# Rebuilding a hybrid decoder layer as a pipeline over four 512-token blocks on eight Trainium2 cores

## The chip, the cores and the metric

The kernel runs on the eight NeuronCores of one Trainium2 (trn2) chip. Each core owns 2048 of the 16384 tokens and also reads the 2048 tokens before its own (the halo), so no core talks to another. The metric is the device time of one launch in microseconds (us), taken as the time of the slowest core. Cores 0 to 3 are one die, cores 4 to 7 the other.

Executions fall in two states. In most, all cores agree within about one per cent (1124.3 to 1131.0 us in the profiled run of the old kernel). In some, the cores of a die run at a lower granted TensorE clock and the time is some per cent longer (in one run of e1 cores 0 to 3 took 1353 to 1369 us at 0.78 to 0.79, cores 4 to 7 1232 to 1247 us at 0.90); such a run is called slow. The engines are named as in the profile: PE is TensorE's matmul, PEld its weight load, DVE VectorE, ACT ScalarE, POOL GpSimd, SP SyncE.

## The reference, cut to what matters

```python
D_MODEL = 1024; SEQ = 16384; HEAD_DIM = 64
ATTN_GROUPS = ((128, 1), (512, 4), (2048, 16))  # (window, dilation) per head group
HEADS_PER_GROUP = 4                             # 12 heads, q, k, v each 768 wide
POOL_WINDOWS = (2, 4, 8, 16)                    # POOL_WIDTH = 256
FFN_HIDDEN = 2816

# one layer, cut
h = rms_norm(x, g_pre_mix[l])
proj = h @ w_in[l]                 # q, k, v (768 each), u (256), gates (2 x 1024)
q = apply_rope(q); k = apply_rope(k)
# ... per group: causal band of 129 positions inside each residue stream, softmax;
#     head j of the three groups is combined, weighted by softmax denominators
o_attn = jnp.sum(wts[..., None] * jnp.stack(outs, axis=0), axis=0)      # 256 wide
y_pool = multiscale_pool(u, w_pool_mix[l], pool_scale[l])               # 256 wide
merged = gate_a * (o_attn @ w_proj_attn[l]) + gate_p * (y_pool @ w_proj_pool[l])
x = x + rms_norm(merged @ w_out[l], g_post_mix[l])
h2 = rms_norm(x, g_pre_ffn[l])
gu = h2 @ w_gate_up[l]
x = x + rms_norm((jax.nn.silu(a) * b) @ w_down[l], g_post_ffn[l])
```

The combination over groups is the same as summing, over the three groups, the unnormalised outputs and the denominators, and dividing once at the end. Both kernels do that. The matmul operands are bf16, accumulation is in f32.

## The kernel before

It works stage by stage over all 2048 tokens, with a barrier of all engines after most stages: the halo is loaded, normalised, transposed and projected while the core's own tokens are loaded; then q and k with rope; then pooling and v; then attention; then the softmax normalisation; the gated merge; the output projection; and the feed-forward network (FFN). Each operation is given its waits by hand.

The statistics of a tile are issued one or two tiles ahead (`lag`) of its scaled copy, and while own tokens are processed the reciprocal root is taken off GpSimd (`rstd_mode["act"]`):

```python
def rstd_chain(ev_ss, col):
    if rstd_mode["act"]:
        e1 = act.op(lambda e: e.activation(out=msA[:, col:col + 1], in_=ssA[:, col:col + 1], func=AF.Sqrt, scale=1.0 / D, bias=EPS), waits=[ev_ss])
        return dve.op(lambda e: e.reciprocal(out=rsA[:, col:col + 1], in_=msA[:, col:col + 1]), waits=[e1])
    e1 = pool.op(lambda e: e.tensor_scalar(out=msA[:, col:col + 1], in0=ssA[:, col:col + 1], scalar1=1.0 / D, scalar2=EPS,
                                           op0=ALU.mult, op1=ALU.add), waits=[ev_ss])
    e2 = pool.op(lambda e: e.tensor_tensor(out=rsA[:, col:col + 1], in0=msA[:, col:col + 1], in1=nhalf[:, :], op=ALU.pow), waits=[e1])
    return e2

def norm_transpose_tile(ev_ld, gvec, dst, dst_col, idx):
    xb = idx % pa_nxb[0]
    xin = xst[xb]
    col = ss_col[0] % 48
    ss_col[0] += 1
    ev_sq = sq_accum(xin[:, :], col, [ev_ld])
    ev_rs = rstd_chain(ev_sq, col)
    n = pa_state["n"]
    pa_state["n"] += 1
    pa_state["q"].append((xin, xb, col, ev_rs, gvec, dst, dst_col, n % 2, n))
    while len(pa_state["q"]) > pa_state["lag"]:
        pa_stage2(pa_state["q"].pop(0))

hTh = P.sb("hTh", [128, 8, 2048], BF16, R_Q)
phase_a(xh, HT // 128, gpre, hTh, pq_from=9, nxb=NXB_MAX, lag=2)      # NXB_MAX = 10 tiles of x
# ... (cut)
pa_state["all_act"] = True
rope_state["qb_dve"] = True
rstd_mode["act"] = True
phase_a(xo, NT, gpre, hT, between=between)
```

Rope uses a matmul with a rotation matrix, then two VectorE products and one GpSimd sum. Attention is a unit per group, stream quarter and head, two units in flight:

```python
for slot in range(4):
    # ... (cut): the score matmuls have 64 rows, 128 columns
    pe.op(lambda e, slot=slot, qs=qs, kc=kc, g=g, p0=p0, pr=pr, bC=bC: e.matmul(ps[:, bC, slot * 128:(slot + 1) * 128], lhsT=kT[g][p0:p0 + 64, pr, kc],
                                                      rhs=qT[p0:p0 + 64, 2 * g + pr, qs], start=True, stop=True), signal=False)
    # ... (cut): the same for the previous block
ev_ec = act.op(lambda e, ub=ub, bC=bC: e.activation(out=PTc[ub][:, :], in_=ps[:, bC, :], func=AF.Exp, scale=0.125),
               waits=[evs, pt_free[ub]])
# ... (cut)
ev_mc = dve.op(lambda e, ub=ub: e.tensor_tensor(out=PTc[ub][:, :], in0=PTc[ub][:, :], in1=masks[:, MC, :], op=ALU.mult), waits=[ev_ec])
# ... (cut)
att_q.append((g, s_, h, ub, ev_mc, ev_mp))
while len(att_q) > 2:
    att_finish(att_q.pop(0))
```

The reciprocal of the denominators is taken as ln and exp on one row per head, split into a high and a low bf16 part and spread over 64 partitions by matmuls with a row of ones (`norm_rows`, `norm_apply`, `norm_pack`).

The softmax here doesn't subtract the row's maximum and nothing guards it: scores larger than these inputs give would overflow.

## Time and profile before

The median is 1132.49 us (two runs, 1131.86 and 1133.12). The view of the whole span first: three rows of the table of 40 equal slices (28.3 us each). A digit is the busy share in tenths; PEclk is the granted TensorE clock in tenths of full speed; DMA is the busy share of the DMA engines.

```profile
PE   2568899999799779999999599999999999999993
PEclk9989899989655559999999789999999999999997
DMA  8996100000000123522088466666333544440231
```

TensorE is at 90% or more in most slices; the exceptions are the first five (the load), three 7s from the start of attention to the normalisation, the 5 at the end of the output projection, and the last slice. Where PEclk shows 5 TensorE is busy but at half clock. The table of stretches of the same core, cut where the lines of code change, gives the stages. The columns are: stretch, its length, then busy us (and instructions) of PE, PEld, DVE, ACT, POOL, the granted clock, the DMA share and GB/s.

```profile
0.00:125.00 125.00, 71.78 (x548) 51.22 (x548) 72.64 (x119) 65.89 (x105) 46.35 (x72) 0.94 0.80 200
125.00:222.00 97.00, 94.46 (x424) 41.81 (x425) 60.44 (x92) 27.70 (x47) 77.91 (x45) 0.97 0.07 23
222.00:290.00 68.00, 62.17 (x466) 48.66 (x464) 19.19 (x22) 26.83 (x63) 22.21 (x8) 0.95 0.00 1
290.00:390.00 100.00, 92.89 (x768) 75.79 (x768) 71.89 (x129) 63.55 (x118) 0.00 (x0) 0.51 0.00 1
390.00:423.00 33.00, 21.35 (x48) 6.86 (x48) 23.28 (x28) 14.94 (x8) 18.44 (x8) 0.50 0.28 49
423.00:566.00 143.00, 140.38 (x640) 63.08 (x640) 41.48 (x65) 39.51 (x65) 48.12 (x47) 0.98 0.26 45
566.00:651.00 85.00, 68.43 (x384) 33.07 (x384) 39.16 (x32) 51.69 (x80) 62.18 (x83) 0.89 0.71 217
651.00:1131.00 480.00, 459.04 (x2112) 207.02 (x2112) 81.30 (x104) 71.65 (x121) 83.24 (x112) 0.98 0.45 94
```

The reader should see where there is something to gain. Attention (290 to 390) keeps TensorE busy but at clock 0.51; the normalisation (390 to 423) likewise, with 21 us of work in 33; the load (0 to 125) has 72 us of matmul in 125. Rope, merge and FFN are already dense at nearly full clock (0.97 to 0.98). The half clock is visible in single instructions. Two lines of the timeline (start us, duration us, engine, line, operation, tiles, sizes) from the attention stage show score matmuls of 128 columns that start 0.10 to 0.11 us apart:

```profile
300.01 0.31 PE L808 MATMUL ps<-qT_62,kT_17_59 64*128 64x128 bf16 x1
300.11 0.31 PE L810 MATMUL ps<-qT_62,kT_17_59 64*128 64x128 bf16 x1
```

### The profile page before, as it was taken

Reading aid. Unit: us, or ns where it says so; the run is one execution under the profiler, and the core shown is the slowest. Engines: PE = TensorE matmul, PEld = TensorE weight load, DVE = VectorE, ACT = ScalarE, POOL = GpSimd, SP = SyncE. Lnnn points to the kernel's source line nnn. Section 1 sums busy time; section 2 is a strip of 40 time slices with the busy share of each in tenths; the row PEclk is TensorE's granted clock in tenths of the full one; section 3 lists DMA queues with packets and bytes.
Section 4 is the critical chain, followed back from the end, with each engine's and each line's share of the span. In section 5 each row is a group of like instructions: output and inputs, shape, how many; then the busy total and the mean of one; then the engine's idle time right before and its main releaser. Section 6 shows DMA issues by size and latency. Waiting matters only on the chain.

```text
span 1131.0 us, 15270 instructions; the slowest of 8 cores (1124.3 to 1131.0 us)
## 1 busy us (share of the span) xinstructions
PE 1010.5 (89%) x5388; PEld 527.5 (47%) x5388; DVE 409.4 (36%) x589; ACT 361.8 (32%) x604; POOL 358.4 (32%) x373
## 2 busy tenths in 40 slices
PE   2568899999799779999999599999999999999993
PEld 1336544359688524444444244444444444444441
DVE  3557566632269772232336412111111121111110
ACT  6535333234775532222247611111111111111110
POOL 3344288805000154323268611111133200000332
PEclk9989899989655559999999789999999999999997
DMA  8996100000000123522088466666333544440231
GB/s 274 219 221 154 55 20 19 1 1 1 2 1 2 19 40 60 89 38 38 1 251 244 157 114 117 115 117 114 57 112 112 130 75 75 77 77 14 95 114 71
DMA packets 32874, 98.79 MB, mean 87 GB/s; under 512 B 4832, under 2 KB 5152, under 8 KB 32800
## 3 DMA queue, kind: packets, MB, share of 16 engines
q0 software_dynamic: 15376, 42.08, 22.3%
q1 hardware_dynamic: 16704, 55.71, 15.3%
q8 instruction: 44, 0.72, 0.3%
q14 instruction: 30, 0.25, 0.1%
q10 hardware_dynamic: 720, 0.03, 0.0%
HBM read 123.10 MB, written 16.78 MB: 124 GB/s over the span
## 4 chain that ended last, share of the span: by engine, by line
PE 79%; DMA 5%; issue 4%; DVE 4%; ACT 4%; POOL 3%; ACTq 0%; SPq 0%; DVEq 0%; POOLq 0%
PE ps L1165 13%; PE ps L1141 13%; PE ps L1144 13%; PE ps L463 9%; PE ps L564 5%; PE ps L949 5%; PE ps L952 5%; DMA sin_43_85<-sint 2%; PE ps L775 2%; PE ps L808 2%; PE ps L810 2%; PE ps L777 2%; PE ps L1009 1%; DVE hTh_92 L411 1%; PE ps L958 1%
## 5 line engine op out<-in xcount | busy, mean ns | idle before, releaser
L1165 PE MATMUL ps<-wdn_133,ffT_151 128*128 128x512 bf16 x704 | 152.3, 379 | 1.9 <-DVE ffT_151 L1149 1.9
L1165 PEld LDWEIGHTS ps<-wdn_133,ffT_151 128*128 128x128 bf16 x704 | 68.8, 98 | 85.4 <-issue 2.8
L463 PE MATMUL ps<-hT_58,wqk_64 128*128 128x512 bf16 x384 | 92.7, 387 | 1.7 <-DVE hT_58 L411 1.7
L1149 DVE TENSOR_TENSOR ffT_151<-ps,sa_113_155 128x512 bf16<-128x512 f32 x44 | 30.4, 691 | 123.0 <-PE ps L1144 123.0
L1149 DVE TENSOR_TENSOR ffT_151<-ps,sa_114_156 128x512 bf16<-128x512 f32 x44 | 30.4, 692 | 121.8 <-PE ps L1144 121.8
L1148 ACT ACTIVATE sa_114_156<-ps 128x512 f32<-128x512 f32 x44 | 26.3, 597 | 125.6 <-PE ps L1141 125.6
L1148 ACT ACTIVATE sa_113_155<-ps 128x512 f32<-128x512 f32 x44 | 26.3, 597 | 121.1 <-PE ps L1141 121.1
L1009 PE MATMUL ps<-wout_131,mT_122 128*128 128x512 bf16 x256 | 58.9, 387 | 2.7 <-POOL mT_122 L970 2.7
L463 PEld LDWEIGHTS ps<-hT_58,wqk_64 128*128 128x128 bf16 x384 | 38.0, 99 | 48.6 <-issue 5.4
L365 POOL TENSOR_SCALAR msA_53<-ssA_52 128x1 f32<-128x1 f32 x64 | 12.1, 190 | 141.6 <-ACT junk_0_105_147 L383 82.5
L1141 PE MATMUL ps<-hT_58,wgu_110_152 128*128 128x512 bf16 x224 | 52.9, 379 | 0.6 <-DMA wgu_110_152<-wgu 0.6
L1141 PE MATMUL ps<-hT_58,wgu_112_154 128*128 128x512 bf16 x224 | 52.9, 379 | 0.0
L1144 PE MATMUL ps<-hT_58,wgu_111_153 128*128 128x512 bf16 x224 | 52.9, 379 | 0.0
L1144 PE MATMUL ps<-hT_58,wgu_112_154 128*128 128x512 bf16 x224 | 52.9, 379 | 0.0
L1141 PE MATMUL ps<-hT_58,wgu_111_153 128*128 128x512 bf16 x224 | 52.9, 379 | 0.0
L1144 PE MATMUL ps<-hT_58,wgu_110_152 128*128 128x512 bf16 x224 | 52.9, 379 | 0.0
L383 ACT ACTIVATE junk_0_105_147<-ps 128x1024 bf16<-128x1024 f32 x23 | 23.3, 1012 | 85.6 <-PE ps L1165 73.8
L564 PE MATMUL ps<-wvr_65,hT_58 128*128 128x256 bf16 x384 | 42.1, 273 | 0.0
L564 PEld LDWEIGHTS ps<-wvr_65,hT_58 128*128 128x128 bf16 x384 | 40.5, 119 | 1.7
L1009 PEld LDWEIGHTS ps<-wout_131,mT_122 128*128 128x128 bf16 x256 | 24.9, 99 | 31.8 <-issue 5.4
L367 POOL TENSOR_TENSOR rsA_54<-msA_53,nhalf_55 128x1 f32<-128x1 f32 x64 | 35.5, 554 | 9.9 <-POOL msA_53 L365 0.8
L74 POOL DMA_DIRECT2D wpa_105<-wpa x1 | 0.6, 574 | 117.6 <-DVE onesb_121 L856 117.6
(272 smaller groups left out, 1895.4 us busy)
## 6 DMA issues: line engine op xcount, KB each, us to landing
wgu_112_154<-wgu POOLq DMA_DIRECT2D x14, 512.0 KB, 5.3
wgu_110_152<-wgu POOLq DMA_DIRECT2D x14, 512.0 KB, 5.3
wgu_111_153<-wgu POOLq DMA_DIRECT2D x14, 512.0 KB, 5.3
wdn_133<-wdn POOLq DMA_DIRECT2D x22, 256.0 KB, 6.1
xin_93_135<-x1s SPq DMA_DIRECT2D x8, 512.0 KB, 4.3
out<-x1b_97_139 SPq DMA_DIRECT2D x8, 512.0 KB, 2.9
xin_94_136<-x1s SPq DMA_DIRECT2D x8, 512.0 KB, 4.1
out<-x1b_98_140 SPq DMA_DIRECT2D x8, 512.0 KB, 2.9
```

The source lines that it names most:

```text
L367: e2 = pool.op(lambda e: e.tensor_tensor(out=rsA[:, col:col + 1], in0=msA[:, col:col + 1], in1=nhalf[:, :], op=ALU.pow), waits=[e1])
L383: ev = act.op(lambda e: e.activation(out=jl[k][:, :], in_=in_ap, func=AF.Square, accum_out=ssA[:, col:col + 1]), waits=list(waits) + [st[" ...
L463: ev = pe.op(lambda e, k=k: e.matmul(ps[:, bank, 0:n], lhsT=wfn(k), rhs=rhsfn(k), start=(k == 0), stop=(k == 7)), signal=(k == 7))
L564: ev = pe.op(lambda e, k=k: e.matmul(ps[:, bank, 0:256], lhsT=tok_ap_fn(k), rhs=wv_tile[:, g, k, :], start=(k == 0), stop=(k == 7)), signa ...
L949: e1 = pe.op(lambda e, k=k, wb=wb, b1=b1, tok=tok: e.matmul(ps[:, b1, :], lhsT=wgs[wb][:, 0, k, :], rhs=hT[:, k, tok], start=(k == 0), sto ...
L952: e2 = pe.op(lambda e, k=k, wb=wb, b2=b2, tok=tok: e.matmul(ps[:, b2, :], lhsT=wgs[wb][:, 1, k, :], rhs=hT[:, k, tok], start=(k == 0), sto ...
L1009: ev = pe.op(lambda e, k=k, hf=hf, pr_=pr_: e.matmul(ps[:, pr_[0] + hf, :], lhsT=mT[:, k, i * 128:(i + 1) * 128], rhs=wout[:, k, hf * 512: ...
L1141: e1 = pe.op(lambda e, k=k, wbuf=wbuf, ba=ba, tok=tok: e.matmul(ps[:, ba, :], lhsT=wbuf[:, 0, k, :], rhs=hT[:, k, tok], start=(k == 0), st ...
L1144: e2 = pe.op(lambda e, k=k, wbuf=wbuf, bb=bb, tok=tok: e.matmul(ps[:, bb, :], lhsT=wbuf[:, 1, k, :], rhs=hT[:, k, tok], start=(k == 0), st ...
L1148: es = act.op(lambda e, ub=ub, ba=ba: e.activation(out=sa[ub][:, :], in_=ps[:, ba, :], func=AF.Silu), waits=[e1, sa_free[ub]])
L1149: ef = dve.op(lambda e, ub=ub, bb=bb, j=j, b=b: e.tensor_tensor(out=ffT[:, j, b * 512:(b + 1) * 512], in0=ps[:, bb, :], in1=sa[ub][:, :], ...
L1165: ev = pe.op(lambda e, j=j, h2=h2, pr_=pr_, il=il: e.matmul(ps[:, pr_[0] + h2, :], lhsT=ffT[:, j, il * 128:(il + 1) * 128], rhs=wdn[:, j, ...
```

## The change

The intent is to mix what is starved (attention) with what is dense (projections, gates, merge), so that TensorE always has dense matmuls to run while ScalarE and VectorE work on the softmax, and to drop the barriers, the rotation matmuls and the serial normalisation. The core's own tokens come first, then the halo; the dilation-16 group, which needs all tokens, is woven with the first block's projections; then attention of block s is woven with the projections of block s+1, the pooling of block s and the merge of block s−1. Rope keeps the two halves of a head in separate tiles, so it needs four products and two sums but no matmul; a score is the sum of two matmuls over 32 rows, one per half. Waits are no longer written by hand: a helper records what each operation reads and writes and derives them.

The full diff replaces most of the file; this is its core, added lines only, with cuts marked. What is removed are the stages described above.

```diff
+def weave(main, fill):
+
+    tm = sum(c for c, _ in main) or 1e-9
+    tf = sum(c for c, _ in fill)
+    fi = 0
+    done_f = 0.0
+    done_m = 0.0
+    for c, fn in main:
+        fn()
+        done_m += c
+        while fi < len(fill) and done_f + fill[fi][0] / 2 <= tf * done_m / tm:
+            fill[fi][1]()
+            done_f += fill[fi][0]
+            fi += 1
+    while fi < len(fill):
+        fill[fi][1]()
+        fi += 1
  ... (cut)
+    def rstd(ss, rs):
+        pool.tensor_scalar(out=ss, in0=ss, scalar1=D * EPS, scalar2=None, op0=ALU.add)
+        pool.tensor_tensor(out=rs, in0=ss, in1=nhalf[:, :], op=ALU.pow)
  ... (cut)
+    def x_stat(i):
+        ss, rs = stat_slot()
+        act.activation(out=junk[:, :], in_=xst[i % 4][:, :], func=AF.Square, accum_out=ss)
+        rstd(ss, rs)
+        sq[i] = rs
+
+    def x_trans(i):
+        xb = xsb[i % 2]
+        act.activation(out=xb[:, :], in_=xst[i % 4][:, :], func=AF.Copy, scale=sq[i])
  ... (cut: the rest of x_trans: eight transposes, then one VectorE evacuation into hT or hTh)
+    def rope(banks, wa, wb, rhs, tab, dst_a, dst_b, view, n=512, t0=0):
+
+        ba, bb = banks.get(), banks.get()
+        pA, pB = ps[:, ba, 0:n], ps[:, bb, 0:n]
+        cos, sin = tab[:, 0, t0:t0 + n], tab[:, 1, t0:t0 + n]
+        ts = [rt[i][:, 0:n] for i in range(4)]
+        mm8(ba, n, wa, rhs)
+        dve.tensor_tensor(out=ts[0], in0=pA, in1=cos, op=ALU.mult)
+        dve.tensor_tensor(out=ts[1], in0=pA, in1=sin, op=ALU.mult)
+        mm8(bb, n, wb, rhs)
+        dve.tensor_tensor(out=ts[2], in0=pB, in1=sin, op=ALU.mult)
+        dve.tensor_tensor(out=ts[3], in0=pB, in1=cos, op=ALU.mult)
+        pool.tensor_tensor(out=dst_a, in0=view(ts[0]), in1=view(ts[2]), op=ALU.subtract)
+        pool.tensor_tensor(out=dst_b, in0=view(ts[1]), in1=view(ts[3]), op=ALU.add)
  ... (cut)
+    x_stat(0)
+    for i in range(2 * NT):
+        if i + 1 < 2 * NT:
+            x_stat(i + 1)
+        x_trans(i)
+        if i + 4 < 2 * NT:
+            x_load(i + 4)
  ... (cut: after each tile: up to two waiting q/k/v units are issued)
+    def att_qk(pair, items, mask):
+
+        pt = PT[pt_i[0] % 2]
+        pt_i[0] += 1
+        n_it = len(items)
+        for j, (kf, qf, c0, n) in enumerate(items):
+            for half in range(2):
+                for hh in range(2):
+                    h = 2 * pair + hh
+                    pe.matmul(ps[:, S_b + hh, c0:c0 + n], kf(half, h), qf(half, h), start=(half == 0), stop=(half == 1),
+                              signal=(j == n_it - 1 and half == 1 and hh == 1), skip_group_check=True)
+        act.activation(out=pt[:, :, :], in_=ps[:, S_b:S_b + 2, :], func=AF.Exp, scale=0.125)
+        dve.tensor_tensor(out=pt[:, :, :], in0=pt[:, :, :], in1=masks[:, mask, :].unsqueeze(1).to_broadcast([128, 2, 512]), op=ALU.mult)
+        return pt
  ... (cut)
+        def fin(pair, n, pt, pv):
+            att_pv(pair, pt, pv, n == 0)
+            if n == 3:
+                a = acc[:, s, 2 * pair:2 * pair + 2, :]
+                dve.tensor_tensor(out=a, in0=ps[:, O_b:O_b + 2, :], in1=a, op=ALU.add)
+                od = oT2[s % 2]
+                for hh in range(2):
+                    h = 2 * pair + hh
+                    vals, sums = (slice(0, 64), slice(64, 128)) if hh == 0 else (slice(64, 128), slice(0, 64))
+                    dve.reciprocal(out=rec[vals, :], in_=acc[sums, s, h, :])
+
+                    dve.scalar_tensor_tensor(out=od[vals, pair, :].rearrange("p (j rho) -> p rho j", rho=4), in0=acc[vals, s, h, :].rearrange("p (rho j) -> p rho j", rho=4),
+                                             scalar=0.5, in1=rec[vals, :].rearrange("p (rho j) -> p rho j", rho=4), op0=ALU.mult, op1=ALU.mult)
+
  ... (cut: u_units: the shifted sums of pooling, in the four blocks)
+            b = fb.get()
+            pe.matmul(ps[:, b, :], wmixb[:, c, :], zT[:, :], start=True, stop=True)
+            act.activation(out=yp[s % 2][:, c, :], in_=ps[:, b, :], func=AF.Copy, scale=pscale[:, c:c + 1])
+        return [(1.8, lambda: proj(0)), (1.8, lambda: proj(1)), (0.1, lambda: sums(0)), (0.1, lambda: sums(1))]
  ... (cut)
+    def wg_load():
+        n = wg_n[0]
+        if n < 32:
+            pool.dma(wgs[n % 2][:, :, :, :], wg_d[n % 8], d_wg[n % 2])
+            wg_n[0] += 1
  ... (cut)
+    weave(g2_main(), f1_units(0, fb))
  ... (cut)
+    for s in range(4):
+        f = []
+        if s < 3:
+            f.append(f1_units(s + 1, fb))
+        f.append(u_units(s))
+        if s > 0:
+            f.append(m_units(s - 1))
+        weave(att_main(s), mix(*f))
  ... (cut)
+    for hf in range(2):
+        pool.dma(wout[:, 4 * hf:4 * hf + 4, :], wout_d[:, 4 * hf:4 * hf + 4, :], d_wo[hf])
  ... (cut)
+    weave(m_units(3), w_units(0, 8, fb))
```

## The prediction

> **What bounds the kernel now.** The table of stretches of the slowest core splits 1131 us (stages cut where the lines change in the timeline) into: input norm, transposes and halo projections 0–125; q/k projections with rope 125–222; pooling and v 222–290; attention 290–390; softmax normalisation 390–423; gated merge 423–566; output projection 566–651; FFN 651–1131. In rope, merge and FFN TensorE is the limit: a 512-column matmul every 0.216 us at granted clock 1.0 (8 take 1.73 us in the chain). These gain nothing. The first 80 us are DMA-bound (DMA share about 1.0, 205–313 GB/s). Attention is TensorE at half clock (granted 0.50, 128-column matmuls 0.106 us apart) with VectorE nearly as full (36.9 of 40 us; 1.05 us accumulation plus 2 x 0.425 us masks a unit). Normalisation is a serial row chain (ln and exp 1.9 us each on one partition). The output projection has 55 us of matmul in 85 us.
>
> [...] the FFN's first eight matmuls take 3.57 us, later ones 1.73.
>
> **Removed:** 48 rotation matmuls in the rope stage (10 us) and their ScalarE copies; hi/lo broadcast and pack matmuls and row chain (33 us stage); all barriers; most idle TensorE around attention. **Added:** scores become two 32-row halves, 672 matmuls against 384; rope has four VectorE products (0.69 us each) instead of a copy and two; its four temporaries are single-buffered behind two 2.1 us GpSimd adds. **Moved:** own tokens first, then halo; attention woven with q/k/v, pool and merge matmuls; output projection woven with merge and FFN.
>
> **Estimate, TensorE stream at full clock from the 0.216 us matmul:**
> - Load phase: 27 MB at the 235–245 GB/s of the first 80 us is about 115 us, with only four x buffers; then about 28 us tail of halo v and last k/v. About 143 us (this includes 41 us of own q/k/v work).
> - Woven attention: 4 x 20.8 (q/k/v) + 16 (pool) + 3 x 34.5 (merge) + 48 x 1.28 (scores and values) = 264 us. Group-2 steps have little dense fill, so clock perhaps 0.75 there: 295 us.
> - Last merge plus half the output projection: 66 us, plus about 22 us of bubbles: wout's load is issued only after the last attention block; the FFN's first weights and hidden tile 7 wait for a norm chain of about 12 us.
> - FFN 456 us plus second half of the output projection 32 us, load hiccups 5, final norm and store 12.
>
> Sum 1026. Tail and bubbles may overlap more than I count, and the pairs of 32-row score matmuls on different row groups may run side by side ([...] this trace shows none), which would save up to 20 us. Central value 1005 us: gains about 70 us in attention and normalisation, 45 in load/rope/pool, 10–20 in output projection; FFN unchanged.
>
> **What would show it:** stretches: FFN half of 44 units 152 us and down 76 us as before; granted clock above 0.9 in woven blocks with merge fill, lower in the first (group 2) block; TensorE idle mostly in the first 115 us, before the output projection and before the FFN; waits there for DMA wout/wgu and for x tiles.
>
> **What would make it wrong:** half clock through group 2 and block 0 (up to +70 us); VectorE stalled in order behind GpSimd's rope adds, starving PSUM banks; on the other side, a load phase under 110 us and no bubbles (down to 950).
>
> Predicted 1005 us, 8 in 10 between 962 and 1055. Faster by over 2%: 0.95; within 2%: 0.04; slower: 0.01.

The sum stands as 1026 (its terms add to 1031, see below); the central value of 1005 takes off some 20 us, for overlap of tail and bubbles and for 32-row score matmuls that run side by side. No trace that the prediction had showed these doing so, and it does not say how their 20 us were worked out; the trace after shows 16 of them in 0.55 us. The clock of 0.75 in group 2 is an estimate of which it gives no working either; it lies between the 0.51 of attention and the 0.98 of the merge in the table above.

## More of the kernel before

The gate weights are loaded once, eight loads of 512 KB, because each is used for all four token blocks in turn; `wout` is loaded during the merge, in eight slices behind the second gate load. The pool-mix matmuls are issued behind the 48 v projections, so the VectorE and GpSimd sums that they need have that time to finish.

## The result, and the profile after

The new kernel takes 1289.06 us (median of two runs, 1285.66 and 1292.45), against 1132.49: the ratio is 1.1385, with a 95% interval from 1.1312 to 1.1458. It is slower by 14%. Here and below the ratios and intervals are worked out from the fast runs; they differ by up to 0.002 from the quotient of the medians (here 1.138). The result is correct.

The same three rows, one slice being 32.3 us here:

```profile
PE   1545566988639858776748959997999999999994
PEclk9777566778869888897977979998999999999997
DMA  8324932003012221333445754544983244442122
```

The first seven slices, where the old kernel was dense from the fourth on, are half empty, and the DMA digits drop to 3 and 2 in the second and third: the DMA engines are mostly idle there, so their rate is not the limit. (HBM reads rose from 123.10 to 150.37 MB, by the page. The 24 more gate loads of 512 KB account for 12.6 MB of that; where the rest comes from was not looked into.) The table of stretches, with the new kernel's stages: the load of own and halo tokens (two halves), group 2 and the four blocks in four pieces, the output projection, the FFN.

```profile
0.00:128.00 128.00, 55.11 (x264) 26.92 (x264) 43.02 (x52) 39.77 (x56) 52.11 (x76) 0.81 0.47 126
128.00:256.00 128.00, 88.33 (x544) 63.13 (x544) 36.73 (x48) 43.65 (x78) 35.73 (x44) 0.66 0.40 94
256.00:362.00 106.00, 83.74 (x788) 50.65 (x782) 62.76 (x63) 45.72 (x57) 34.19 (x20) 0.82 0.14 25
362.00:468.00 106.00, 72.86 (x452) 36.63 (x452) 61.35 (x68) 22.67 (x36) 34.55 (x28) 0.86 0.26 42
468.00:574.00 106.00, 77.62 (x462) 38.08 (x462) 61.00 (x62) 23.32 (x37) 32.56 (x26) 0.86 0.25 45
574.00:681.00 107.00, 64.73 (x372) 29.29 (x373) 66.47 (x60) 23.16 (x33) 20.18 (x22) 0.79 0.38 78
681.00:771.00 90.00, 70.55 (x342) 31.73 (x342) 30.38 (x31) 34.60 (x55) 46.32 (x57) 0.88 0.60 149
771.00:1290.00 519.00, 492.09 (x2304) 224.44 (x2304) 101.33 (x120) 97.29 (x161) 109.79 (x140) 0.97 0.44 99
```

No engine is full in any of the first six stretches: VectorE's largest share is 66 of 107 us, TensorE's 84 of 106. So the loss is in waits, and the view of the waits says which. For PE in the first 245 us (engine, tile awaited, line; us in total, times, longest):

```profile
PE ps L94 <- ACT xsb_30_72 L92: 70.1, 15, 8.8
PE ps L94 <- ACT xsb_29_71 L92: 31.8, 8, 15.7
```

and for PE from 256 to 672 us:

```profile
PE ps L92 <- DVE zT_112 L92: 59.2, 7, 15.5
PE ps L94 <- DVE PT_53_95 L92: 14.0, 5, 10.2
PE ps L94 <- DMA wgs_55_97<-wg: 13.4, 4, 4.7
```

**The load phase.** `xsb` is the scaled copy of an x tile, waiting to be transposed. Why does it come late? The timeline of one round:

```profile
66.69 1.90 POOL L92 TENSOR_TENSOR q_19_61<-rt_48_90,rt_50_92 128x512 bf16<-128x512 f32 x1 [9.15 <-DVE rt_50_92 L92]
68.54 1.90 POOL L92 TENSOR_TENSOR q_19_61<-rt_49_91,rt_51_93 128x512 bf16<-128x512 f32 x1
...
70.77 0.57 POOL L92 TENSOR_TENSOR rs_53<-ss_52,nhalf_51 128x1 f32<-128x1 f32 x1
...
71.44 1.15 ACT L92 ACTIVATE xsb_30_72<-xst_23_65,rs_53 128x1024 bf16<-128x1024 f32 x1 [10.45 <-POOL rs_53 L92]
72.73 0.90 PE L94 MATMUL ps<-ident_43,xsb_30_72 128*128 128x128 bf16 x7 [6.89 <-ACT xsb_30_72 L92]
```

The bracket is the idle time before the instruction and what ended it. The copy needs the reciprocal root `rs`; that is a GpSimd operation of 0.57 us which stands in GpSimd's queue behind the two rope sums, 1.90 us each; those wait for VectorE's products, which wait for matmuls, which stand in TensorE's queue behind the transposes of the tile before. The statistics run one tile ahead, the rope units come every second tile, and work runs in the order of its queue (shown for GpSimd at the end of this paragraph), so the round closes on itself. These copies (every second tile) start at 43.30, 56.72, 71.44, 84.45, 100.29 and 114.23: 14 us for two tiles of 512 KB each. The trace shows the order of GpSimd's queue: the work for `rs` runs only after both sums, from 70.40 us, although the square sum that it needs was read out on ScalarE by 58.91, before the sums began at 66.69.

Could it be the x tiles that come late? The waits of ScalarE in the first 256 us say no. It waits 95.6 us for `rs` (77.1 in the first line below, 18.5 for the other copy buffer), but for x tiles only 14.8, all of it in the first 28 us (the second line is the largest part):

```profile
ACT xsb_30_72 L92 <- POOL rs_53 L92: 77.1, 9, 11.6
ACT junk_73 L92 <- DMA xst_22_64<-xo: 7.6, 1, 7.6
```

**The woven blocks.** `zT` is the input of the pool-mix matmul. VectorE's timeline before the longest of the seven waits:

```profile
371.42 3.35 DVE L92 RECIPROCAL rec_113<-acc_56 64x512 f32<-64x512 f32 x1
374.88 1.28 DVE L92 SCALAR_TENSOR_TENSOR oT_0_62_104<-acc_56,rec_113 64x512 bf16<-64x512 f32 x1
376.19 3.35 DVE L92 RECIPROCAL rec_113<-acc_56 64x512 f32<-64x512 f32 x1
...
380.97 0.71 DVE L92 TENSOR_TENSOR uY_110<-uX_67_109 128x527 f32<-128x527 f32 x1
...
387.22 0.58 PE L92 MATMUL ps<-zT_112,wmixb_50 128*128 128x512 bf16 x1 [15.53 <-DVE zT_112 L92]
```

Two reciprocals and two products of a head pair, then the pooling sums, then the matmul: it is issued directly behind them, and everything behind it on TensorE waits too, for 15.53 us. The group of reciprocals, as the page has it (busy us, mean ns, idle before):

```profile
L92 DVE RECIPROCAL rec_113<-acc_56 64x512 f32<-64x512 f32 x16 | 53.6, 3347 | 1.1
```

54 us of VectorE that the prediction did not price at all.

**The clock.** The granted clock is 0.66 in the second stretch, and 0.69 from 350 to 400 us: it is low in the stretches where the longest waits are 8.8 to 15.7 us, and it recovers to 0.97 in the FFN. In the 2.5 us after a wait for `zT` it was 0.50 to 0.57 six times, after waits of 4.6 to 15.5 us, and 1.00 twice, after waits of 1.8 us. The length of the wait does not settle it: after six waits for the gate weights it was 0.52 to 0.64 four times (1.7, 2.6, 2.9 and 4.7 us) and 1.00 twice (2.7 and 3.4 us). Nor are waits the whole of it: in the old kernel's attention the clock was 0.50 from 300 to 340 us, where the profile has TensorE busy for all 40 us.

**What came as predicted.** The 32-row score matmuls do run side by side. Two lines of the timeline after, in a dense stretch: eight of the sixteen matmuls of one step, in two groups of four,

```profile
404.73 0.28 PE L94 MATMUL ps<-q_1_41_83,k_1_38_80 32*128 32x128 bf16 x4
404.85 0.27 PE L94 MATMUL ps<-q_1_41_83,k_2_39_81 32*128 32x128 bf16 x4
```

and the next operation's first matmul starts at 405.28: 16 matmuls in 0.55 us, 34 ns each, where 128 columns one after the other, scaled from the measured 0.216 us for 512 columns, would take about 54 ns each (my estimate from that duration). In the same trace value matmuls of 128 rows and 128 columns do start 57 ns apart (the eighth at 294.20 us, the first at 293.80, clock 1.00).

### The profile page after: what moved, and what is told of

Read it like the earlier page. It is cut to its first block, busy times and chain, and to the rows that moved or that the text cites. A ratio compares the mean times of both kernels' runs of the same rounds, so it can differ in the third digit from the quotient of the medians.

```text
span 1290.6 us, 14962 instructions; the slowest of 8 cores (1275.2 to 1290.6 us)
## 1 busy us (share of the span) xinstructions
PE 1005.0 (78%) x5520; PEld 500.9 (39%) x5520; DVE 463.0 (36%) x502; ACT 330.2 (26%) x511; POOL 365.4 (28%) x410
## 3 DMA queue, kind: packets, MB, share of 16 engines
HBM read 150.37 MB, written 16.78 MB: 130 GB/s over the span
## 4 chain that ended last, share of the span: by engine, by line
PE 63%; DVE 11%; DMA 8%; POOL 6%; issue 6%; ACT 6%; DVEq 0%; ACTq 0%; POOLq 0%; SPq 0%
PE ps L94 56%; PE ps L92 7%; DVE rec_113 L92 4%; DMA wgs_55_97<-wg 2%; DMA wgs_54_96<-wg 2%; POOL k_20_62 L92 1%; DMA wout_115<-wout 1%; DVE zT_112 L92 1%; ACT xsb_30_72 L92 1%; DVE rt_50_92 L92 1%; ACT junk_73 L92 1%; DMA xst_22_64<-xo 1%; POOL rs_53 L92 1%; DMA pscale_47<-pscale 1%; POOL q_19_61 L92 1%
## 5 line engine op out<-in xcount | busy, mean ns | idle before, releaser
L94 PE MATMUL ps<-wdna_133,ffT_132 128*128 128x512 bf16 x512 | 115.7, 379 | 0.0
L94 PE MATMUL ps<-hT_54,wgu_87_129 128*128 128x512 bf16 x420 | 102.7, 385 | 3.4 <-DMA wgu_87_129<-wgu 3.4
L94 PE MATMUL ps<-hT_54,wgu_88_130 128*128 128x512 bf16 x420 | 100.4, 379 | 0.0
L94 PE MATMUL ps<-hT_54,wgu_89_131 128*128 128x512 bf16 x392 | 94.5, 381 | 0.0
L94 PEld LDWEIGHTS ps<-wdna_133,ffT_132 128*128 128x128 bf16 x512 | 50.1, 98 | 60.4
L94 PE MATMUL ps<-hT_54,wgs_55_97 128*128 128x512 bf16 x224 | 60.7, 417 | 15.0 <-DMA wgs_55_97<-wg 14.4
L92 POOL TENSOR_SCALAR ss_52<-ss_52 128x1 f32<-128x1 f32 x80 | 17.8, 222 | 180.6 <-ACT junk_85_127 L92 118.3
L92 ACT ACTIVATE junk_85_127<-ps 128x1024 bf16<-128x1024 f32 x32 | 32.7, 1021 | 138.6 <-PE ps L92 138.6
L94 PE MATMUL ps<-ident_43,xsb_30_72 128*128 128x128 bf16 x112 | 13.3, 288 | 70.1 <-ACT xsb_30_72 L92 70.1
L94 PE MATMUL ps<-hT_54,wgs_54_96 128*128 128x512 bf16 x224 | 61.4, 419 | 6.8 <-DMA wgs_54_96<-wg 6.7
L94 PEld LDWEIGHTS ps<-hT_54,wgu_87_129 128*128 128x128 bf16 x420 | 41.5, 99 | 54.1 <-issue 6.6
L92 PE MATMUL ps<-zT_112,wmixb_50 128*128 128x512 bf16 x8 | 4.1, 506 | 73.0 <-DVE zT_112 L92 73.0
L94 PEld LDWEIGHTS ps<-hT_54,wgu_88_130 128*128 128x128 bf16 x420 | 41.0, 98 | 49.1
L94 PEld LDWEIGHTS ps<-hT_54,wgu_89_131 128*128 128x128 bf16 x392 | 38.5, 98 | 46.4 <-issue 1.1
L92 DVE RECIPROCAL rec_113<-acc_56 64x512 f32<-64x512 f32 x16 | 53.6, 3347 | 1.1
L92 DVE TENSOR_TENSOR ffT_132<-ps,sa_93_135 128x512 bf16<-128x512 f32 x30 | 20.8, 692 | 86.9 <-PE ps L92 86.9
L92 POOL TENSOR_TENSOR rs_53<-ss_52,nhalf_51 128x1 f32<-128x1 f32 x80 | 45.4, 567 | 16.3 <-DVE nhalf_51 L92 4.6
L92 DVE TENSOR_TENSOR ffT_132<-ps,sa_94_136 128x512 bf16<-128x512 f32 x29 | 20.1, 692 | 82.1 <-PE ps L92 82.1
L92 DVE TENSOR_TENSOR ffT_132<-ps,sa_95_137 128x512 bf16<-128x512 f32 x29 | 20.1, 691 | 80.7 <-PE ps L92 80.7
L92 DVE TENSOR_TENSOR PT_53_95<-PT_53_95,masks_44 128x1024 bf16<-128x1024 bf16 x24 | 34.0, 1418 | 17.6 <-ACT PT_53_95 L92 17.6
L94 PE MATMUL ps<-wdnb_134,ffT_132 128*128 128x512 bf16 x160 | 39.8, 379 | 0.0
L92 ACT ACTIVATE sa_94_136<-ps 128x512 f32<-128x512 f32 x29 | 17.3, 597 | 87.4 <-PE ps L92 87.4
```

Source lines behind the costliest of these rows:

```text
L92: self.ops.append(lambda e: getattr(e, method)(*args, **kw).then_inc(sem, 1))
L94: self.ops.append(lambda e: getattr(e, method)(*args, **kw))
```

## The experiments

All are edits of the new kernel. The first four each test one suspected cause alone; the rest build up. A gain is quoted as the difference of two ratios to the old kernel, times 1132 us, because the calls ran on different chips and each had its own runs of the old kernel (medians of the fast ones 1131.9, 1132.9, 1132.3 and 1131.7). By the intervals, a gain over the new kernel, of which there are only two runs, is sure to about 9 us, and one between two later runs to 3 or 4 us. For the stages, single profiles are compared: three edits that don't touch the load phase (e2, e3, e4) still show its end, the first exponential, at 252 to 253 us in place of 256, so differences of 4 us there mean nothing.

The two theories: **(T)** the loss is in-order waiting that the new order of issue created, in places that can be named (the x-tile round, the pool-mix matmul, the reciprocals, the weight loads), and the woven plan is sound; **(R)** the plan itself is at fault: the load phase is DMA-bound or limited by its four x buffers, and the woven blocks are limited by the total work of VectorE or by the half clock, so mending single waits brings little.

### e1_stat: statistics two tiles ahead

```diff
+    x_stat(1)
-        if i + 1 < 2 * NT:
-            x_stat(i + 1)
+        if i + 2 < 2 * NT:
+            x_stat(i + 2)
```

> The square sum and rstd of an x tile are issued two tiles ahead instead of one. Theory A (the load phase of about 250 us is a loop through the in-order queues: transposes wait for ScalarE, which waits for the GpSimd rstd that stands behind the rope adds of the previous projection, which stand behind the projection's matmuls, 14 us for two tiles): the loop is broken, two tiles take about 8 us, the load phase falls to about 170 us and the total by 60 to 90 us. Rival B (the load phase is limited by DMA or by having only four x buffers): no more than 15 us change.

Measured: ratio 1.106 (1.1038 to 1.1082), 37 us less than the new kernel; the first exponential starts at 218 us in place of 256. The direction is right, the size is a miss. The page shows a second round that the first had hidden. ScalarE in the halo half of this run:

```profile
111.94 0.38 ACT L92 ACTIVATE v<-ps 128x256 bf16<-128x256 f32 x1 [1.32 <-PE ps L92]
112.22 1.05 ACT L92 ACTIVATE junk<-xst 128x1024 bf16<-128x1024 f32 x1
...
113.25 1.14 ACT L92 ACTIVATE xsb<-xst,rs 128x1024 bf16<-128x1024 f32 x1
```

The next tile's square (`junk`) and this tile's copy (`xsb`) stand behind the evacuation of a v projection, which waits for TensorE, which has that projection behind the transposes of the tile before. So the copy too has to be issued ahead of the units (e5). In this run ScalarE also waits 36 us for x tiles after the first have landed, so rival R has some part in what is left.

### e2_late: the pool-mix matmul issued later

```diff
+    zT1 = P.sb("zT1", [128, 512], BF16, take(KB))
+    zTs = [zT, zT1]
...
+        def mixmm(c):
             b = fb.get()
-            pe.matmul(ps[:, b, :], wmixb[:, c, :], zT[:, :], start=True, stop=True)
+            pe.matmul(ps[:, b, :], wmixb[:, c, :], zTs[c][:, :], start=True, stop=True)
...
-        return [(1.8, lambda: proj(0)), (1.8, lambda: proj(1)), (0.1, lambda: sums(0)), (0.1, lambda: sums(1))]
+        return [(1.0, lambda: proj(0)), (1.0, lambda: proj(1)), (0.1, lambda: sums(0)), (0.1, lambda: sums(1)),
+                (2.0, lambda: mixmm(0)), (0.6, lambda: mixmm(1))]
```

> The pool-mix matmul of a block is issued some 10 us of fill work after the sums that feed it, with a second zT buffer, instead of straight behind them. Theory A (TensorE stands in order at this matmul, 73 us in all in the trace of the changed kernel, most of it lost, and the clock falls to half after each): 50 to 75 us faster. Rival B (the woven blocks are bound by VectorE, busy 15 to 20 of 25 us in many stretches, so the idle time only moves): under 20 us.

Measured: 1.1066 (1.1039 to 1.1093), 36 us less. This is less than theory A's 50 to 75 us and more than the rival's 20: part of the wait was real loss, part only moved. All waits for `zT` are gone, 59 us of them in the woven blocks and 14 just after, and 36 come back as time. The rest turned into other waits: TensorE now waits 31 us for the gated products `tg` in these blocks, where it waited 11 before, and 18 us for `wout`, where it waited 4.

### e3_copy: reciprocals replaced by copies (wrong result)

```diff
-                    dve.reciprocal(out=rec[vals, :], in_=acc[sums, s, h, :])
+                    dve.tensor_copy(out=rec[vals, :], in_=acc[sums, s, h, :])
```

> Wrong result on purpose: each of the 16 reciprocals of 64x512 (3.35 us each, 53.6 us of VectorE) becomes a copy. Theory A (VectorE's long instructions hold up the bank releases and the pool sums behind them): 20 to 40 us faster, because part of the wait on zT goes with it. Rival B (VectorE is off the critical path): under 8 us.

Measured: 1.0912 (1.0894 to 1.0931), 54 us less. The sixteen copies take 0.422 us each against 3.347, an eighth, so 46.8 us of VectorE work were removed, and the time fell by about as much (54 with an uncertainty of 9): this work is on the critical path almost one to one, although VectorE is busy only about 60% of the woven stretches. The gain was more than expected, and about half of it may be the wait for `zT`, which falls from 73 to 48 us in this run.

### e4_wgs3: a third buffer for the gate weights

```diff
-    wgs = [P.sb("wgs%d" % i, [128, 2, 8, 128], BF16, R2 + i * 4 * KB) for i in range(2)]
+    wgs = [P.sb("wgs%d" % i, [128, 2, 8, 128], BF16, (R2 + i * 4 * KB) if i < 2 else R2 + 43 * KB + 256) for i in range(3)]
...
-            if j == 1 and wg_n[0] == m_n[0] + 1:
+            if j == 1 and wg_n[0] == m_n[0] + 2:
```

> A third buffer for the gate weights, loaded two units ahead. Theory A (about 20 us of TensorE waits on the gate weights' DMA, and slow clock after each, 4.4 per cent of the chain): 15 to 40 us faster. Rival B (the waits only stand in for VectorE or pool waits that follow): under 8 us.

Measured: 1.1265 (1.1177 to 1.1353), an interval that overlaps the new kernel's own (1.1312 to 1.1458); its fast runs were 1266.9 and 1283.88, the other two were slow. Inconclusive by itself: the gain lies between nothing and some 25 us. The profile of the faster run does show the wait itself gone: 21.1 us for the gate weights in the new kernel, none here.

### e5_ahead: statistics two tiles ahead, scaled copy one tile ahead

```diff
+    def x_copy(i):
+        act.activation(out=xsb[i % 2][:, :], in_=xst[i % 4][:, :], func=AF.Copy, scale=sq[i])
...
+        if i + 1 < 2 * NT:
+            x_copy(i + 1)
+            if i + 5 < 2 * NT:
+                x_load(i + 5)
         x_trans(i)
-        if i + 4 < 2 * NT:
-            x_load(i + 4)
```

(on top of e1)

> As e1_stat, and the scaled copy of an x tile is also issued one tile before its transposes. e1's trace showed a second loop in the halo half of the load phase: ScalarE's square and copy of the next tile stand behind the evacuations of the two v projections, which stand behind the transposes that need the copy, 6.9 us a tile. If the remaining loss of the load phase is this loop (theory A), the first score exponential starts at about 165 us or earlier, against 218 in e1 and 256 in the changed kernel, and the total is 40 to 60 us below e1 (about 1200). If it is DMA or the four x buffers (rival B), it starts after 205 and the total is within 15 us of e1.

Measured: 1.0809 (1.078 to 1.0838), 65 us less than the new kernel, 28 less than e1. The first exponential starts at 191.7 us. The order of issue alone, with the same four x buffers and the same bytes, shortens the load phase from 256 to 192 us; so neither the DMA rate nor the number of buffers set the 256, and rival R falls as the main cause in this phase. (A copy issued earlier also frees its x buffer earlier, so the loads start sooner; the run doesn't separate this.) It did not come down as far as expected, 165 us: TensorE still waits 53 us for `xsb`, and ScalarE 60 us for `rs`.

### e6_late: e5 and e2 together

The edit is that of e2, on top of e5.

> e5 and the late pool-mix matmul of e2. If load phase and woven blocks are separate losses, the 35 us of e2 add to e5 in full; if both only move the work to a shared limit, less than 20.

Measured: 1.0532 (1.0509 to 1.0555), 31 us less than e5. Alone (e2) the same edit gave 36: the two causes lie in different stages and add nearly in full.

### e7_rec: one reciprocal for two heads, with the right result

```diff
-                a = acc[:, s, 2 * pair:2 * pair + 2, :]
-                dve.tensor_tensor(out=a, in0=ps[:, O_b:O_b + 2, :], in1=a, op=ALU.add)
...
-                    dve.reciprocal(out=rec[vals, :], in_=acc[sums, s, h, :])
...
+                    dve.tensor_tensor(out=rec[vals, :], in0=ps[sums, O_b + hh, :], in1=acc[sums, s, h, :], op=ALU.add)
+                    dve.tensor_tensor(out=val[vals, :], in0=ps[vals, O_b + hh, :], in1=acc[vals, s, h, :], op=ALU.add)
+                dve.reciprocal(out=rec[:, :], in_=rec[:, :])
```

(then one product for both heads; on top of e6)

> e6 and one reciprocal for two heads instead of two (right result): 7.4 us of VectorE a pair instead of 10.5 by the durations of the trace, 25 us less over 8 pairs. If VectorE limits the woven blocks (e3 gave back 54 us for 54 us of reciprocals less about 6 of copies), 20 to 30 us faster than e6; if e3's gain was mostly the wait of the pool-mix matmul, which e6 has already taken away, under 10.

Measured: 1.0292 (1.0275 to 1.031), 27 us less than e6, as expected, and correct. VectorE's busy time falls by 24.6 us (460.3 to 435.7), so its work counts about one to one here too, with the wait for `zT` already gone. The group of reciprocals in this run:

```profile
L92 DVE RECIPROCAL rec<-rec 128x512 f32<-128x512 f32 x8 | 26.8, 3353 | 0.2
```

128 partitions cost what 64 did (3353 ns against 3347), so putting the denominators of two heads side by side halves the cost.

### e8_early: the output-projection and first FFN weights loaded early, in large pieces

```diff
+        if s == 3:
+            d_wo = [dsem("d_wo%d" % i) for i in range(2)]
+            for hf in range(2):
+                pool.dma(wout[:, 4 * hf:4 * hf + 4, :], wout_d[:, 4 * hf:4 * hf + 4, :], d_wo[hf])
...
+    for _ in range(3):
+        gu_load()
+    weave(w_units(0, 8, fb, 3.0), m_units(3))
```

(on top of e7)

> e7, with the output projection's weights and the first FFN weights issued before the stage that needs them, and the last merge units spread to the end of that stage. The stage between the last attention block and the FFN is about 92 us long for 66 us of matmul; expected 15 to 25 us faster than e7.

Measured: one fast run of 1168.81 us, the other three slow; the fast run shows no gain over e7 (1167.0). The waits say why. In e7 TensorE waits 13.9 us for `wout`, 5.0 for the FFN weights and 25.7 for the gate weights. Here the first two are gone and the third has grown:

```profile
PE ps L94 <- DMA wgs<-wg: 48.7, 14, 16.4
```

The 2 MB of `wout` (as bf16) were issued from GpSimd at 472.4 and 472.9 us, in front of gate weights that were needed sooner; from 480 to 490 us the DMA share is 1.00 and the other engines are busy for 0.00 us. The wait was exchanged, not removed: the stretch before the output projection is 6 us shorter than in e7, the output projection 11 us longer. A miss against the 15 to 25 us expected.

### e9_rstd: the reciprocal root of the load phase on ScalarE

```diff
         act.activation(out=junk[:, :], in_=xst[i % 4][:, :], func=AF.Square, accum_out=ss)
-        rstd(ss, rs)
+        act.activation(out=ss, in_=ss, func=AF.Ln, bias=epsb[:, :])
+        act.activation(out=rs, in_=ss, func=AF.Exp, scale=-0.5)
```

(on top of e7; `epsb` holds the constant D·eps)

> e7, with the rstd of the load phase computed on ScalarE (ln and exp on one column) instead of GpSimd. e7 still shows 60 us of TensorE waiting for the scaled x tile in its load phase, 17 us for four tiles, where ScalarE waits for a GpSimd rstd that stands behind two 1.9 us rope adds. If that queueing is what is left (theory A): first score exponential at 165 to 175 us against 191, total 15 to 25 us below e7. If the four rope temporaries or the DMA hold the phase (rival B): under 8 us. [...]

Measured: 1.018 (1.0164 to 1.0196), 13 us less than e7; the first exponential at 179.3 us, 12 earlier. It falls between theory A (15 to 25 us) and the rival (under 8): GpSimd's queue still mattered after e5, but it was not all that was left. The profile shows three table loads (`ACT_TABLE_LOAD`) on ScalarE, 1.28 us each, against two in e7, so they cost little here.

### e10_spread: a third gate buffer, and wout in small slices between the gate loads

```diff
-            if j == 1 and wg_n[0] == m_n[0] + 1:
+            if j == 1 and wg_n[0] == m_n[0] + 2:
...
+            if s == 2 and j == 0:
+                pool.dma(wout[:, c, :], wout_d[:, c, :], d_wo[c])
...
+            if s == 3 and j == 0 and c in (5, 6, 7):
+                gu_load()
...
-    weave(m_units(3), w_units(0, 8, fb))
+    weave(w_units(0, 8, fb, 3.0), m_units(3))
```

(on top of e7, with the third buffer of e4; `zT` moved into the `yp` tiles to make room)

> e7 with a third gate-weight buffer, the output projection's weights loaded in eight slices during the last attention block, the first FFN weights during the last merge units, and the merge units spread to the end of that stage. e8 loaded early in large pieces and only moved the wait to the gate weights in the same queue (20.7 and 19.9 us). If the DMA waits of this stage are real losses, not just exchanged ones, 20 to 35 us below e7 (1132 to 1147); if exchanged, within 8 us of e7.

Measured: 0.9952 (0.9935 to 0.997), 38 us less than e7. The waits for gate weights are gone entirely (25.7 us in e7), and those for `wout` and the FFN weights went from 18.9 to 9.1. Of the 38 us, 37 lie in the stretch between the first exponential and the output projection, where 22 us of gate waits and 10 of `wout` waits went away. The run bundles the third buffer, the slices and the order of the last units, so what the buffer, which could not be seen in e4, is worth alone is not shown.

### e11_both: e9 and e10 together, six rope temporaries in the load phase

```diff
+    rtx = [P.sb("rtx%d" % i, [128, 512], F32, R6 + i * 2 * KB) for i in range(2)]
...
-        ts = [rt[i][:, 0:n] for i in range(4)]
+        pool_ = rt + rtx if banks is pj else rt
+        ts = [pool_[(rt_i[0] + i) % len(pool_)][:, 0:n] for i in range(4)]
```

(and the edits of e9 and e10)

> e9 and e10 together, and six rope temporaries instead of four in the load phase. If the losses are separate: 35 to 60 us below e7, about 1110 to 1130, faster than the kernel before the change; if they share a limit, above 1140.

Measured: 1107.92 us median, correct; ratio 0.9787 (0.9769 to 0.9804). It is 57 us faster than e7, 6 more than e9 and e10 give singly (not separable from noise, so the two temporaries show no effect of their own). It is 24 us faster than the old kernel and 181 us faster than the new one; whether the gain over the old one exceeds 2% the interval leaves just open. Its two rows:

```profile
PE   1776688795999989986988999799999999999993
PEclk9989898897999999987999999899999999999997
```

and its stretches of load and woven blocks:

```profile
0.00:174.00 174.00, 112.57 (x808) 74.12 (x808) 78.13 (x101) 97.82 (x199) 63.88 (x55) 0.93 0.61 162
174.00:498.00 324.00, 278.92 (x2056) 148.60 (x2057) 215.48 (x251) 114.51 (x160) 125.03 (x100) 0.91 0.32 59
```

The woven blocks now run at clock 0.91 with TensorE busy 279 of 324 us.

### e12_seq: e11 without the weaving

```diff
-    weave(g2_main(), f1_units(0, fb))
+    for _, fn in g2_main() + f1_units(0, fb):
+        fn()
...
-        weave(att_main(s), mix(*f))
+        for _, fn in att_main(s) + mix(*f):
+            fn()
```

> e11_both without the interleaving: in each woven stretch the attention steps run first and the projection, pool and merge units after them; nothing else changes, the result stays right. It asks what the interleaving, which was the change's main intent, is worth once the queue faults are mended. Theory A (the interleaving hides the exponential, mask and reciprocal behind dense matmuls): the stretch from the first exponential to the first output-projection matmul grows from 324 us to 365-405 us, the time goes from 1108 us to 1145-1190 us, and the granted clock falls towards 0.5-0.7 in the attention parts. Rival B (the stretch is bound by the sum of VectorE's work and by the unit order, so interleaving no longer matters): within 15 us of 1108 us.

Measured: 1160.62 us median, correct; 1.0254 (1.0232 to 1.0276), 53 us more than e11. The stretches of load and blocks in this run:

```profile
0.00:173.00 173.00, 109.91 (x808) 73.42 (x808) 78.16 (x101) 97.80 (x198) 63.42 (x55) 0.93 0.61 163
173.00:555.00 382.00, 312.83 (x2061) 171.77 (x2056) 196.34 (x255) 115.20 (x160) 117.57 (x100) 0.79 0.28 53
```

The load phase is the same; the blocks take 382 us in place of 324, at clock 0.79 in place of 0.91 (0.61 in the first 57 us, where group 2 now runs alone, with 0.50 from 185 to 215, and 0.54 to 0.58 in the attention parts of the four blocks). Theory A of this run holds in each number. TensorE's busy time itself grows from 279 to 313 us, 34 of the 58: by the profile, much of what weaving saves is matmuls at a low clock. The weaving, the main idea of the change, works and is worth 53 us once the faults around it are mended; they cost 181 us together and hid it. What the weaving was worth in the new kernel before it was mended was not tested.

## Why the prediction was wrong

The direction and the size were both wrong: 1005 us predicted, 962 to 1055 as the range, 1289 measured. The terms of its sum, set against the stages of the new kernel and of e11 (marks: first exponential, first output-projection matmul, first FFN matmul; 256.3, 681.0 and 771.5 us in the new kernel, 173.9, 498.2 and 590.2 in e11). The terms as written add to 1031, not 1026, a slip of 5 us.

| term of the prediction | us predicted | new kernel | e11 |
|---|---|---|---|
| load phase | 143 | 256 | 174 |
| woven attention | 295 | 425 | 324 |
| last merge, half output projection, bubbles (66 + 22) | 88 | 91 | 92 |
| FFN, second half of the output projection, end (456 + 32 + 5 + 12) | 505 | 519 | 516 |

1. **"Load phase: 27 MB at the 235–245 GB/s of the first 80 us is about 115 us" failed.** It took the old kernel's DMA rate for the new one's limit and never asked who would issue the work of each tile, in which queue, behind what. The new kernel moved 126 GB/s in its first 128 us, with the DMA engines 47% busy. The round through GpSimd and ScalarE set the pace, 14 us for two tiles. e1, e5, e9 and e11 changed only the order, the engine of the reciprocal root and two temporaries, and took the phase from 256 to 174 us. The listed danger was "VectorE stalled in order behind GpSimd's rope adds"; the stalled ones were ScalarE's copy behind the reciprocal root on GpSimd, and TensorE behind the copy. The old kernel's odd-looking switches (statistics a tile or two ahead, reciprocal root off GpSimd, ten x buffers for the halo) fit this danger; the rebuild dropped them, and the prediction counted of them only the buffers. Bringing back the first two in the new kernel gave 65 us (e5) and 13 us (e9); more x buffers were not tried. What keeps the phase at 174 and not 143 is not settled: TensorE still waits 41 us there for `xsb` in e11, and the DMA share is 0.61.
2. **"Woven attention: 264 us, 295 with a lower clock in group 2" failed.** It summed TensorE's stream alone. VectorE's reciprocals (54 us) and the products behind them were not in the sum at all; the order of the pool-mix matmul (59 us of TensorE waits) and the gate weights' two buffers for 32 loads were not looked at. e2 and e6 (36 and 31 us) show the order of the pool-mix matmul as a cause, e3 and e7 (54 and 27) the reciprocals, and e10 (38) the weight loads, these as a bundle. By the marks of the profiles the stretch goes from 425 us (421 in e5) to 385 with e6, 361 with e7 and 324 with e10. That is still 29 more than predicted. Theory R was not wholly wrong here: in e3 and e7 VectorE's work counted about one to one, and the longest waits that are left are for VectorE. e11's waits of PE from 240 to 500 us are led by 16.3 us for the gated products `tg`, 8.1 for `PT` and 7.7 for `val`, all on VectorE.
3. **The clock**: "above 0.9 in woven blocks with merge fill, lower in the first": 0.79 to 0.86 in the new kernel, so wrong there; in e11 0.84 in the first 66 us of the stretch, 0.87 in the next 65 and 0.92 to 0.97 after that, so right once the waits are gone. It was named among what would make the prediction wrong ("half clock through group 2 and block 0, up to +70 us"), but as a cause. In these runs it went with the waits: over the woven stretch it was 0.83 in the new kernel, 0.87 in e6, 0.90 in e7 and 0.92 in e10. But long waits alone don't explain it: it was also low in the attention parts of e12 (0.54 to 0.58) and of the old kernel (0.51).
4. **The listed bubbles** (wout, FFN weights) were real: the chain of waits has 13.9 us of DMA for `wout` at 671.7 us. In the table part of it falls into the woven stage, since the first output-projection matmul lies inside it.
5. **Right**: FFN unchanged in rate; scores in pairs on different row groups, which "this trace shows none" of and which the new trace shows (34 ns each, above); that weaving gains (e12 against e11, 53 us; the prediction had about 70 for attention and normalisation).

One further cost was in neither sum: in these traces VectorE's mask product takes longer when a GpSimd instruction runs at the same time (0.69 us against a mean of 1.51). Three lines of the timeline after: the product with GpSimd idle, then a GpSimd sum, and the product that began 0.84 us after it.

```profile
290.29 0.69 DVE L92 TENSOR_TENSOR PT_53_95<-PT_53_95,masks_44 128x1024 bf16<-128x1024 bf16 x1 [2.04 <-ACT PT_53_95 L92]
...
294.26 2.12 POOL L92 TENSOR_TENSOR q_0_40_82<-rt_48_90,rt_50_92 128x512 bf16<-128x512 f32 x1 [13.32 <-DVE rt_50_92 L92]
...
295.10 1.84 DVE L92 TENSOR_TENSOR PT_52_94<-PT_52_94,masks_44 128x1024 bf16<-128x1024 bf16 x1 [0.38 <-ACT PT_52_94 L92]
```

GpSimd's sum ended at 296.38, and the product at 296.94, 0.56 us later, a little less than its free 0.69. Why it took longer is not shown. Of the 48 products in this trace, the 18 that meet no GpSimd instruction of over 0.9 us take 0.69 us each, the 30 that do average 1.51. In e12, where attention runs apart from most GpSimd sums, the 48 products average 0.712 us; in e11 1.236 (the longest 2.59), so some 25 us of VectorE (48 times 0.52) go this way; in the old kernel GpSimd was idle during attention (0.00 us of 100). What this costs in time was not tested: argued, not shown.

## What to carry to other kernels

When stages are woven together, write down for each engine the order of its queue and follow one tile round it, because each unit that waits in the middle of a queue holds up everything behind it (here for up to 15.5 us, at one pool-mix matmul); a sum of busy times per engine, however careful, can't show this. Issue what releases others (statistics, scaled copies, the next weights) ahead of what fills, and issue a matmul well after the work that feeds it, not behind it. Before calling a plan wrong, mend the waits one at a time: they hide each other (a third weight buffer gave nothing clear alone and helped take 38 us off later), and the idea may be sound underneath.
